# A gated attention and convolution block on one core: raw results of the first three projection pairs, their 1/rms applied in the output projections, and new due stages for the operands of the second half

## The chip, the core and the metric

The kernel runs on one core of one Trainium2 chip. The metric is the device time of one execution in microseconds (us); lower is better. The core's engines are named as in the profile: PE is TensorE (matmuls; PEld its weight loads), DVE is VectorE, ACT is ScalarE, POOL is GpSimd, SP is SyncE, which only issues DMAs. Each engine works through its own queue in order. ACT issues some DMAs too.

## The reference

`x` has 2048 tokens of 1024 features. All is float32. Cut to what matters:

```python
def rmsnorm(x, g):
    r = lax.rsqrt(jnp.mean(x * x, axis=-1, keepdims=True) + EPS)
    return (x * r) * g

h = rmsnorm(x, norm_g)
proj = h @ w_in            # 1024 x 6144
q, k, v, z_att, gb, gc, u, z_conv, g_att, g_conv = split(proj)
att = chunked_rel_attention(q, k, v, rel_bias)   # 64-token chunks, 8 chunks back, 8 heads
y_att = (att * silu(z_att)) @ w_att_out
vconv = causal_depthwise_conv(gc * u, conv_w, conv_b)
y_conv = (gb * vconv * silu(z_conv)) @ w_conv_out
m = sigmoid(g_att) * y_att + sigmoid(g_conv) * y_conv
x = x + m @ w_out
out = rmsnorm(x, final_norm_g)
```

The 6144 columns of `w_in` are 512 each for q to z_conv, and 1024 each for the two gates. Since 1/rms is one factor for each token, it can be applied to `x` before the projection or to the projection's result after it.

## The kernel before, in words

**Number format.** Each float32 operand is split into a high and a low part (`split_into`, `split_pair`): ACT casts the high part (L127, L133), DVE subtracts it from the source to get the low part (L128, L134). A product of two operands takes three matmul passes (`passes`, L140 to L142): high by high, high by low, low by high.

**The projection.** The tokens are worked in two halves of 1024, each in two chunks `c` of 512 columns. The weight columns are worked in 24 pairs `p` of two 128-column tiles `n`. A pair of tiles by two chunks of tokens is a 2x2 block product, done in Strassen's form with Winograd's additions: seven products instead of eight, in the order `ORDER = (1, 2, 6, 7, 4, 5, 3)`. Each product is a "stage": 12 matmuls (four tiles of 128 rows by three passes) into one bank of PSUM. Its operands are combinations of the token blocks, t1 to t7 (tiles t10h, t10l to t73l; built by `operand_steps`, one product's operands for each step), and combinations of the weights (`operand`: tiles `wc`, out of raw weights `wraw`, loaded in pairs). The weight combinations of half 0 are stored in DRAM (the `wc` stores) and loaded again for half 1 (L383), except those of the first three pairs in the order.

**The plain pairs.** Half 0 begins before 1/rms is known. Its first three pairs (`PLAIN = 3`, gate columns d = 0 to 2 of g_att and g_conv, tiles `n` = 0 and 1) are computed without Strassen on tokens that are multiplied by the norm's gain only (`raw_split`): 12 products `q`, each of 24 matmuls, into banks `ps_p`. Meanwhile the sums of squares and 1/rms are made (`rb`, one tile for each chunk), and DVE normalizes the tokens (`normalize`, `third`). The results of the first four plain products are copied by ACT; those of the others stay in their bank. Each is then multiplied by 1/rms on DVE (`scaled`, L654), after which `ev_gate` does a tanh on ACT (L416) and stores the gate through ACT's own DMA queue (L417). In between, operand steps of half 0 (t1, t2, t6, t7, t4) and the first weight combinations are built. All this is under a schedule written by hand for PE, DVE and ACT, so the order of the code is the order on the engines.

**The change of halves.** The last pair of half 0 (z columns) and the pair before it are interleaved, then the first two pairs of half 1 (`ending`, `beginning`). In these, the operands t1 to t7 are rebuilt from the tokens of half 1, into slots that half 0's operands leave. `turned = operand_steps(1)` is advanced one step each time a stage `s` reaches the first entry of the list `due`. Before, each of the last pair's seven stages adds an entry two stages later. With S the stage of the first product of the last pair, the steps come at S + 3, 4, 5, 7, 9, 11 and 13. The last z results (`sz`, L468, on DVE) are stored by SP (L474), in the same queue as the loads of `wc` (L383) and of raw weights (L375).

**Attention** runs among the projection stages of half 1: scores (`ps_s`), softmax (`nmax`, `rs`, `pr`), transposes, `pt` split into parts on ACT and DVE (L219, L220), and the product with `vv` (L229). At the end of half 1's projections the attention and convolution results of half 0 (`mid`) are loaded by SP into operand slots that come free.

**The output projections** (`half_c`, one for each half of the tokens) go through 16 items (i, d) in the order of `ITEMS_C`: i = 1 is the convolution branch, i = 0 attention, d a 128-column tile. For each item, weights `wy` are split, two gate tiles `gl` are loaded by SP from `gate_d` (L558, a pool of five buffers), and one product of 12 matmuls runs for each chunk. DVE then forms (gate + 1) x product (L960, L963) and adds the two branches (L964). Jobs for the next part, W_out's product in `half_d`, are worked off between: splits of W_out's tiles (`wor`, L903 and L904) and of m (`mix`, L926, L927). PSUM holds three banks for these products.

## Time and profile before

| | |
|---|---|
| time, three runs | 1504.21 us median (1502.57 to 1506.2) |
| the profiled execution's own time | 1508.27 us |
| its span in the trace | 1506.5 us |
| mean granted clock of PE | 0.995 |
| PE busy | 1475.3 us, 98% |
| DVE busy | 1090.5 us, 72% |
| ACT busy | 740.1 us, 49% |
| DMA | 408.28 MB, mean 271 GB/s |

How to read it: times in the trace are us from the span's start. A row of a timeline has the start, the duration, the engine, the line of the kernel, the operation, out<-in with the buffer numbers left out, and the shapes; in square brackets stand the engine's idle time before it and what ended it. "x2" at the end means that two such instructions follow each other without a gap. A row of the waits has the waiting engine and line, the engine and tile that ended the wait, then the us in total, how many times, and the longest. A row of the windows has the stretch, its length, the busy time of each engine asked for with the number of instructions, the granted clock of PE as a share of full speed, the mean share of the DMA engines' time, and GB/s. "DMA to landing" is the time from the issue of a DMA to its landing.

### The profile page before, as it was taken

How to read it: one execution, taken by the hardware profiler on the slowest of the kernel's cores; microseconds unless marked ns; L12 is line 12 of the kernel's file. 1: busy time of each engine (PE TensorE's matmuls, PEld its weight loads, DVE VectorE, ACT ScalarE, POOL GpSimd, SP SyncE). 2: the span in 40 equal slices, each digit the busy share in tenths (PEclk: the TensorE clock that was granted, in tenths of full speed). 3: DMA queues.
4: the chain of work that ended last, by engine and by line, in shares of the span. 5: the costliest groups of instructions: out<-in, count | busy, mean ns of one | idle time of the engine just before them, and what ended most of it. 6: DMA issues, size and time to landing. Idle time of an engine off the chain costs nothing. (4 is left out here: it accounts for less than half of the span.)

```text
span 1506.5 us, 21077 instructions
## 1 busy us (share of the span) xinstructions
PE 1475.3 (98%) x6976; PEld 1226.2 (81%) x6976; DVE 1090.5 (72%) x2121; ACT 740.1 (49%) x1399; POOL 163.8 (11%) x310
## 2 busy tenths in 40 slices
PE   8899999999999999999999999999999999999997
PEld 6778888888877788887888888888888888888886
DVE  7977588596557784676677777787765577767687
ACT  7363453444345333565566666666666223423153
POOL 0000000000000002232222323322220000010000
PEclk9999999999999999999999999999999999999999
DMA  5279899989988895999898887878989845877443
GB/s 214 73 273 352 308 361 351 348 295 328 345 304 287 314 341 173 339 341 337 288 295 286 259 260 249 265 256 264 310 282 314 307 129 168 294 262 240 153 162 112
DMA packets 168748, 408.28 MB, mean 271 GB/s; under 512 B 21056, under 2 KB 41536, under 8 KB 168640
## 3 DMA queue, kind: packets, MB, share of 16 engines
q1 hardware_dynamic: 137008, 316.48, 60.7%
q0 software_dynamic: 22272, 73.42, 15.4%
q10 hardware_dynamic: 9360, 17.04, 3.1%
q8 instruction: 55, 0.90, 0.2%
q14 instruction: 53, 0.43, 0.1%
HBM read 251.67 MB, written 155.19 MB: 270 GB/s over the span
## 5 line engine op out<-in xcount | busy, mean ns | idle before, releaser
L162 POOL DMA_DIRECT2D q<-q x128 | 66.8, 527 | 675.5 <-DVE wc L128 585.0
L204 ACT ACTIVATE pr<-ps_s,nmax 128x640 f32<-128x640 f32 (+4 forms) x128 | 93.5, 730 | 93.0 <-DVE nmax L200 92.3
L206 ACT ACTIVATE pr<-pr,rs 128x640 f32<-128x640 f32 (+4 forms) x128 | 97.9, 765 | 35.3 <-DVE rs L205 34.9
L200 DVE CUSTOM_DVE_ANT_0 ps_s<-ps_s,bs 128x640 f32<-128x640 f32 (+4 forms) x128 | 95.3, 744 | 23.7 <-PE ps_s L194 22.4
L140 PE MATMUL ps_d<-mid,wy 128*128 128x512 f32 x256 | 99.7, 389 | 0.8 <-ACT wy L127 0.8
L128 DVE TENSOR_TENSOR wc<-wraw,wc 128x512 fp32r<-128x512 f32 x120 | 82.3, 688 | 24.7 <-ACT wc L127 24.5
L141 PE MATMUL ps_d<-mid,wy 128*128 128x512 f32 x256 | 99.6, 389 | 0.0
L194 PE MATMUL ps_s<-kk,q 128*128 128x320 f32 (+1 forms) x448 | 98.5, 334 | 1.0 <-ACT pr L204 0.5
L142 PE MATMUL ps_d<-mid,wy 128*128 128x512 f32 x256 | 99.3, 389 | 0.0
L220 DVE TENSOR_TENSOR pt<-ps_t,pt 128x640 fp32r<-128x640 f32 (+4 forms) x128 | 94.1, 735 | 3.4 <-ACT pt L219 2.5
L127 ACT CAST wc<-wraw 128x512 fp32r<-128x512 f32 x120 | 74.1, 621 | 44.2 <-PE ps_c L142 23.0
L219 ACT CAST pt<-ps_t 128x640 fp32r<-128x640 f32 (+4 forms) x128 | 80.1, 626 | 21.9 <-PE ps_t L214 20.7
L214 PE MATMUL ps_t<-ident,pr 128*128 128x128 f32 x560 | 82.3, 273 | 0.2
L229 PE MATMUL po<-pt,vv 128*128 128x512 f32 x336 | 75.5, 356 | 4.1 <-DMA vv<-v 3.2
L229 PEld LDWEIGHTS po<-pt,vv 128*128 128x128 f32 x336 | 62.1, 188 | 19.1 <-issue 3.5
L214 PEld LDWEIGHTS ps_t<-ident,pr 128*128 128x128 f32 x560 | 65.7, 140 | 9.9 <-issue 1.5
L194 PEld LDWEIGHTS ps_s<-kk,q 128*128 128x128 f32 x448 | 67.6, 190 | 5.6 <-ACT pr L204 4.8
L997 PE MATMUL ps_w<-wo,lefth 128*128 128x512 f32 (+1 forms) x240 | 71.9, 382 | 0.0
L140 PEld LDWEIGHTS ps_d<-mid,wy 128*128 128x128 f32 x256 | 48.0, 188 | 11.1 <-ACT wy L127 1.2
L234 DVE TENSOR_TENSOR ot<-po,ot 64x256 f32<-64x256 f32 x64 | 26.6, 415 | 41.3 <-ACT ot L233 40.4
L141 PEld LDWEIGHTS ps_d<-mid,wy 128*128 128x128 f32 x256 | 48.0, 188 | 10.1
L142 PEld LDWEIGHTS ps_d<-mid,wy 128*128 128x128 f32 x256 | 48.1, 188 | 9.9
(535 smaller groups left out, 4110.4 us busy)
## 6 DMA issues: line engine op xcount, KB each, us to landing
wc<-wc SPq DMA_DIRECT2D x294, 512.0 KB, 5.3
wraw<-wp_in SPq DMA_DIRECT2D x54, 512.0 KB, 5.8
q<-q POOLq DMA_DIRECT2D x128, 128.0 KB, 5.0
gl<-gate SPq DMA_DIRECT2D x64, 256.0 KB, 2.8
mid<-mid SPq DMA_DIRECT2D x64, 256.0 KB, 5.3
wor<-wo SPq DMA_DIRECT2D x56, 256.0 KB, 5.2
bs<-bias POOLq DMA_DIRECT2D x32, 320.0 KB, 7.7
v<-vst SPq DMA_DIRECT2D x64, 128.0 KB, 4.6
```

The source lines that it names most:

```text
L128: nc.vector.tensor_sub(w[:, 1], src, w[:, 0].bitcast(F32))
L140: nc.tensor.matmul(ps, lhsT=w[:, 0, k, :], rhs=rh[:, cs], start=(first and not onto and k == 0), stop=False, skip_group_check=onto)
L141: nc.tensor.matmul(ps, lhsT=w[:, 0, k, :], rhs=rl[:, cs], start=False, stop=False, skip_group_check=onto)
L142: nc.tensor.matmul(ps, lhsT=w[:, 1, k, :], rhs=rh[:, cs], start=False, stop=(last and k == len(rhs) - 1), skip_group_check=onto)
L194: nc.tensor.matmul(ps[:, i, :m], lhsT=q[s][:, g * P:(g + 1) * P], rhs=kk[:, k1 - n + i * m:k1 - n + (i + 1) * m], start=(s == 0), stop=(s ...
L200: nc.vector.tensor_tensor_reduce(out=view, in0=view, in1=bv, scale=-0.125, scalar=3.0e38, op0=ALU.add, op1=ALU.min, accum_out=nmax)
L204: nc.scalar.activation(out, view, AF.Exp, bias=nmax, scale=-1.0, accum_out=rs)
L206: nc.scalar.activation(pr[:, :n], pr[:, :n], AF.Identity, scale=rs)
L214: nc.tensor.transpose(out=ps[:, j * P:(j + 1) * P], in_=pr[:, j * P:(j + 1) * P], identity=ident)
L219: nc.scalar.copy(hi[:, js, qs], src)
L220: nc.vector.tensor_sub(lo[:, js, qs], src, hi[:, js, qs].bitcast(F32))
L229: nc.tensor.matmul(ps[:, :, a * P:b * P], lhsT=vv[:, g0 + j, :], rhs=pt[:, j, :, a * P:b * P], start=(i == 0), stop=(i == len(js) - 1))
```

## The change

Three things.

1. The 12 plain results are no longer multiplied by 1/rms and no longer go through `ev_gate`. ACT copies each out of its bank, and SP stores it raw in `plain_d`. SP also stores the two tiles of 1/rms (`rb_d`).
2. In `half_c` of the first half, for items with d < 3, the loaded raw gate is multiplied by 1/rms on DVE and goes through the tanh on ACT, in place. The two 1/rms tiles (`rbs`) are loaded by SP into operand slots, ahead of the first `mid` loads. `ITEMS_C` and the order of `mix` are rearranged.
3. `due` is set once, from the list `TURN`. The seven steps in `ORDER`'s order come at S + 3, 4, 6, 9, 13, 16 and 18.

```diff
+TURN = (2, 3, 5, 8, 12, 15, 17)
...
+    plain_d = [dram.tile([P, CH], F32, name=f"plain{q}") for q in range(4 * PLAIN)]
+    rb_d = [dram.tile([P, CH], F32, name=f"rb{c}") for c in range(2)]
...
     def gate(i, d, c):
         g = gp.tile([P, CH], F32, tag="g", name="gl")
-        nc.sync.dma_start(g, gate_d[i][d][c])
+        nc.sync.dma_start(g, plain_d[plain.index((d, i, c))] if unscaled(d, c) else gate_d[i][d][c])
         return g
 
-    ITEMS_C = [(i, d) for dd in ((0, 4, 1, 5), (2, 6, 3, 7)) for i in (1, 0) for d in dd]
+    def unscaled(d, c):
+        return d < PLAIN and c < 2
+
+    ITEMS_C = [(i, d) for dd in ((3, 7, 0, 4), (1, 5, 2, 6)) for i in (1, 0) for d in dd]
...
-    def scaled(p, n, c, src):
-        t = src if src.space != PSUM else e("c")
-        nc.vector.tensor_mul(t, src, rb[c])
-        late.append(lambda: evs[p][n](c, c, t))
...
-        if q in (6, 7):
-            for n in range(2):
-                copied.pop(0)()
         if q > 5 and len(built) < 5:
             built.append(next(steps))
...
                 rb[0] = inverse(ry[0], e)
+                store(rb_d[0], rb[0])
...
                     rb[1] = inverse(ry[1], e)
+                    store(rb_d[1], rb[1])
                 passes(ps, wops0[p, n, k], [raw_ops[c, 4 * k + j] for j in range(4)], slice(0, CH), k == 0, k == 1)
-            if q < 4:
-                t = e("plain")
-                nc.scalar.copy(t, ps)
-                copied.append(lambda p=p, n=n, c=c, t=t: scaled(p, n, c, t))
-            else:
-                now, late = late, []
-                between(q)
-                if q > 4:
-                    scaled(*held0)
-                held0 = (p, n, c, ps)
-                for fn in now:
-                    fn()
+            t = e("plain")
+            nc.scalar.copy(t, ps)
+            store(plain_d[q], t)
+            between(q)
...
-        scaled(*held0)
-        for fn in late:
-            fn()
...
                 turned = operand_steps(1)
-            due.append(s + 2)
+                due = [s + d for d in TURN]
...
             made = make_c(0, ITEMS_C[0])
+            rbs = [fslot("rbs") for c in range(2)]
+            for c in range(2):
+                nc.sync.dma_start(rbs[c], rb_d[c])
             mids = {c: [load_mid(1, b, c) for b in range(4)] for c in (0, 1)}
...
             split_into(w, raw)
+            if d < PLAIN and not hf:
+                for c in cs:
+                    nc.vector.tensor_mul(gl[c], gl[c], rbs[c])
+                    nc.scalar.activation(gl[c], gl[c], AF.Tanh, scale=0.5)
...
             if n_ in (7, 10, 14, 15):
-                mix((7, 10, 14, 15).index(n_))
+                mix((3, 0, 1, 2)[(7, 10, 14, 15).index(n_)])
```

In the changed kernel the line numbers are three higher in the first part of the program, and from the plain stage on about ten to thirteen lower: L133 becomes L136, L468 becomes L471, and L798 becomes L785. TensorE runs the same matmuls in both.

The order of the instructions changes at these places, among others. On ACT in the plain stage, between the casts of t6 and t7 for half 0, this stands before (plain and c are results of plain products, "DMA gate" is a store that ACT issues):

```order
L133 CAST t63h<-xs 128x512
L416 ACTIVATE plain<-plain 128x512
L417 DMA gate_0_1_156<-plain 128x512
L416 ACTIVATE plain<-plain 128x512
L417 DMA gate_0_1_188<-plain 128x512
L416 ACTIVATE c<-c 128x512
L417 DMA gate_1_1_160<-c 128x512
L133 CAST t70h<-xs 128x512
L133 CAST t71h<-xs 128x512
L133 CAST t72h<-xs 128x512
L133 CAST t73h<-xs 128x512
```

And this in the changed kernel:

```order
L136 CAST t63h<-xs 128x512
L714 COPY plain<-ps_p 128x512
L136 CAST t70h<-xs 128x512
L136 CAST t71h<-xs 128x512
L136 CAST t72h<-xs 128x512
L136 CAST t73h<-xs 128x512
L714 COPY plain<-ps_p 128x512
L136 CAST t40h<-xs 128x512
```

The tanh and the stores have left the queue, and copies out of the banks ps_p stand there.

On DVE at the change of halves, near the end of half 0, this stands before (sz and v are z results of half 0; t4, t5 and the tiles t1 belong to the operands of half 1):

```order
L815 TENSOR_TENSOR v_4827<-v_4827,ps_c_4695 128x512
L134 TENSOR_TENSOR t43l_4808<-xs_1580,t43h_4807 128x512
L362 TENSOR_TENSOR t1_4851<-xs_1586,xs_1577 128x512
L468 SCALAR_TENSOR_TENSOR sz_4830<-sz_4830,v_4827 128x512
L468 SCALAR_TENSOR_TENSOR sz_4848<-sz_4848,ps_c_4433 128x512
L134 TENSOR_TENSOR t50l_4854<-t1_4851,t50h_4853 128x512
L362 TENSOR_TENSOR t1_4857<-xs_1586,xs_1577 128x512
L362 TENSOR_TENSOR t1_4863<-xs_1586,xs_1577 128x512
L362 TENSOR_TENSOR t1_4869<-xs_1586,xs_1577 128x512
L134 TENSOR_TENSOR t51l_4860<-t1_4857,t51h_4859 128x512
L468 SCALAR_TENSOR_TENSOR sz_4890<-sz_4890,ps_c_4546 128x512
```

And this in the changed kernel:

```order
L802 TENSOR_TENSOR v_4807<-v_4807,ps_c_4675 128x512
L137 TENSOR_TENSOR t73l_4788<-xs_1583,t73h_4787 128x512
L361 TENSOR_TENSOR xs_1580<-xs_1580,xs_1577 128x512
L471 SCALAR_TENSOR_TENSOR sz_4810<-sz_4810,v_4807 128x512
L471 SCALAR_TENSOR_TENSOR sz_4828<-sz_4828,ps_c_4433 128x512
L471 SCALAR_TENSOR_TENSOR sz_4846<-sz_4846,ps_c_4546 128x512
L137 TENSOR_TENSOR t40l_4873<-xs_1580,t40h_4872 128x512
```

The last three sz now stand ahead of t4, and t5 follows later in the queue.

On DVE near the end of half 1, among the softmax of attention, this stands before:

```order
L220 TENSOR_TENSOR pt_5674<-ps_t_11636,pt_5674 128x5x128
L205 RECIPROCAL rs_11652<-rs_11652 128x1
L200 ISA ps_s_11681,nmax_11686<-ps_s_11681,bs_11501 128x2x320
L200 ISA nmax_11686 128x1
L220 TENSOR_TENSOR pt_5674<-ps_t_11673,pt_5674 128x5x128
```

And this in the changed kernel, where gl is a raw gate and rbs the tile of 1/rms:

```order
L223 TENSOR_TENSOR pt_5674<-ps_t_11636,pt_5674 128x5x128
L208 RECIPROCAL rs_11652<-rs_11652 128x1
L938 TENSOR_TENSOR gl_11992<-gl_11992,rbs_11881 128x512
L203 ISA ps_s_11681,nmax_11686<-ps_s_11681,bs_11501 128x2x320
L203 ISA nmax_11686 128x1
L223 TENSOR_TENSOR pt_5674<-ps_t_11673,pt_5674 128x5x128
```

The first of the twelve new multiplications stands there. The others are in the output projections of the first half.

On SP in the plain stage, the store of each plain result stands in its own turn: those of the fifth to the eighth result and of the second tile of 1/rms are ahead of the two raw weight loads of the fifth pair, or between them.

More of the change, by code (lines that the diff above doesn't have):

```diff
@@ L642, in block_kernel @@
     plain = [(p, n, c) for p in range(PLAIN) for c in range(2) for n in range(2)]
-    copied = []
-    late = []
     nw = 0
```

## Prediction

> **What bounds the kernel now.** I read the page's first part, then TensorE's waits, then every gap of TensorE on its timeline, then windows of 4 us around the gaps.
>
> ```profile
> span 1506.5 us, 21077 instructions
> PE 1475.3 (98%) x6976; PEld 1226.2 (81%) x6976; DVE 1090.5 (72%) x2121; ACT 740.1 (49%) x1399; POOL 163.8 (11%) x310
> ```
>
> TensorE (PE) works for 1475.3 of 1506.5 us, so the span is its work plus 31.2 us of gaps. The change leaves all matmuls, so it can only win or lose gaps, and time in which the clock is low. The waits say who ends the gaps (us in total, times, longest):
>
> ```profile
> PE ps_p L140 <- DVE c L654: 4.7, 2, 2.9
> PE ps_c L140 <- ACT wc L127: 4.4, 2, 3.2
> ```
>
> The first row and the longest of the second lie in the plain stage, before 90 us. On PE's timeline these and the gaps at the change of halves are:
>
> ```profile
> 58.66 0.66 PE L140 MATMUL ps_p<-rawh,w 128*128 128x512 f32 x1 [1.86 <-DVE c L654]
> 74.27 0.50 PE L140 MATMUL ps_p<-rawh,w 128*128 128x512 f32 x1 [2.87 <-DVE c L654]
> 88.65 0.50 PE L140 MATMUL ps_c<-t10h,wc 128*128 128x512 f32 x1 [3.16 <-ACT wc L127]
> ...
> 493.61 0.50 PE L140 MATMUL ps_c<-t30h,wc 128*128 128x512 f32 x1 [0.54 <-ACT v L814]
> 503.26 0.50 PE L140 MATMUL ps_d<-t20h,wc 128*128 128x512 f32 x1 [0.90 <-DMA wc<-wc]
> 510.84 0.47 PE L140 MATMUL ps_d<-t20h,wc 128*128 128x512 f32 x1 [1.80 <-ACT t33h L133]
> ```
>
> So the change touches two places, with 1.86 + 2.87 + 3.16 = 7.89 us and 0.54 + 0.90 + 1.80 = 3.24 us of gaps. The granted clock (the column PEclk, third from the end) answers to some gaps:
>
> ```profile
> 56.00:60.00 4.00, 2.14 (x8) 0.85 0.30 113
> 60.00:64.00 4.00, 4.00 (x15) 0.73 0.64 197
> 72.00:76.00 4.00, 1.73 (x8) 1.00 0.35 130
> 88.00:92.00 4.00, 3.35 (x9) 0.69 0.90 208
> 92.00:96.00 4.00, 4.00 (x17) 0.89 0.99 385
> ```
>
> After the gap of 1.86 us, 4 x (0.15 + 0.27) = 1.68 us of clock are lost; after that of 3.16 us, 4 x (0.31 + 0.11) = 1.68 us; after that of 2.87 us none. The first loss is hidden, since PE then waits for VectorE anyway; the second is paid.
>
> **Part 1, the plain stage.** The question is when the first Strassen product (88.65 us) can start. It needs t1 to t4 and its weights, all out of one chain on VectorE (DVE) and ScalarE (ACT).
>
> ```profile
> 76.53 0.69 DVE L134 TENSOR_TENSOR t70l<-xs,t70h 128x512 fp32r<-128x512 f32 x1 [2.32 <-ACT t70h L133]
> ...
> 78.95 0.69 DVE L654 TENSOR_TENSOR c<-ps_p,rb 128x512 f32<-128x512 f32 x1
> 79.55 0.68 DVE L358 TENSOR_TENSOR xs<-xs 128x512 f32<-128x512 f32 x1
> ```
>
> ```profile
> 86.96 0.62 ACT L416 ACTIVATE c<-c 128x512 f32<-128x512 f32 x1
> ...
> 87.98 1.14 ACT L127 CAST wc<-wraw 128x512 fp32r<-128x512 f32 x2 [0.40 <-ACT c L416]
> ```
>
> By the order rows shown with the change, three tanh with their DMA issues have gone from ahead of t70h on ACT, for one copy. The terms:
> - Twelve multiplications L654 leave DVE, nine of them ahead of t43l; one row starts 0.60 us after the one before (78.95, 79.55). 9 x 0.60 = -5.4 us.
> - The wait of 2.32 us for t70h, which those three tanh made, goes: the copy in their place belongs to a product that has ended by then. -2.3 us.
> - A tanh and its issue stand ahead of the weight cast that PE waits for: 87.98 - 86.96 = -1.0 us.
> - The copy of the eighth product stands ahead of t20h and holds t2 back: +0.7 us, an estimate.
> - A new wait. The raw weights of the fifth pair are loaded when the last plain weights are split, before here:
>
> ```profile
> 59.75 5.74 SPq L375 DMA_DIRECT2D wraw<-wp_in  x2
> ```
>
> The second went out 0.3 us before the end of these 5.74 us, at 65.2; with seven of the multiplications gone ahead of it and the 0.7 us it is 65.2 - 4.2 + 0.7 = 61.7 now. SyncE's queue (SP) is in order, and four plain stores (plain4 to plain7) and a store of 1/rms are queued ahead of those two loads. I cost them at nothing: the last needs the copy of the eighth product, which ends at 58.66 - 1.86 = 56.8, plus 0.6 for the copy. Loads of wraw take this long here, between 50 and 80 us and between 40 and 130 us:
>
> ```profile
> DMA to landing us min/median/max: 3.6/3.7/3.7
> ...
> DMA to landing us min/median/max: 3.6/6.2/7.3
> ```
>
> With 3.7 us the pair lands at 65.4; DVE, counted on at 0.60 us a row, comes to it (L392) at 64.6, and t6 and t4 are queued behind it. I take +0.9 us (0 to 4.4, with 7.3).
>
> Sum: -5.4 - 2.3 - 1.0 + 0.7 + 0.9 = -7.1 us; the product of 88.65 us starts at 81.5. PE itself would now be there earlier: without waits at 58.66 and 74.27, since ACT empties the banks by then, the last four plain products run on from 56.8, 24 matmuls or 5.44 us each (twice the product measured in part 3), to 78.6. A gap of some 2.9 us stays. If the clock drops after it, the 1.68 us are paid as before, and the gain is 7.1; if not, it is 8.8. Gaps of 1.86 and 3.16 us had a drop, the one of 2.87 none: I take the drop, as the gap is nearest in its place and releaser to the one of 3.16.
>
> The Trainium skill (TensorE: Matmul & The Clock Gate, Part 1) has the clock halved after an idle window of about 3.4 us, windows running freely. Half rate for 3.4 us is the measured 1.7 us. But it also says that idle gaps only matter above 3.4 us, and the gaps of 1.86 and 3.16 us here speak against that; by its rule the sum of this part would be 8.8, which is a rival below.
>
> **Part 2, the change of halves.** The operand steps of half 1 were due two stages after each product of the last pair, now at fixed stages with the later ones (t4, t5, t3) further out.
>
> ```profile
> 505.00:510.00 5.00, 5.00 (x10) 1.00 0.93 334
> ```
>
> ```profile
> 502.68 0.32 SPq L474 DMA_DIRECT2D z<-sz  x1
> ...
> 504.06 0.38 SPq L383 DMA_DIRECT2D wc<-wc  x1
> ```
>
> ```profile
> 506.16 0.69 DVE L468 SCALAR_TENSOR_TENSOR sz<-sz,ps_c 128x512 f32<-128x512 f32 x1
> ```
>
> DVE (second number) never rests there. The z results wait in its queue behind operands, SP's z stores wait for them, and weight loads stand behind those stores. The gap at 510.84 is named after t33h, which that product doesn't read; its weights were issued at 504.06. By DVE's order rows at the change of halves, the last sz moves up past t5, t4 and the tiles t1: counted in the whole order by eleven rows (11 x 0.60 = 6.6 us), the third last by six (3.6 us). With the store of that one the load of 504.06 moves to about 500.5. Its weights then land 3.6 us earlier, more than the 1.80 us that PE waited. Since PE arrives earlier too, I leave 1.0 of the 3.24 us standing: -2.2 us (-3.2 to -0.5). What is deferred is needed late: half 1's first pair runs two products for each of t1, t2, t6, t7 and t4 before it reads t5 and t3.
>
> **Part 3, what is added later.** Two loads of 1/rms stand on SP ahead of the loads of the attention results, and wait for the first operand slots to come free:
>
> ```profile
> 1143.47 1.37 SPq L553 DMA_DIRECT2D mid<-mid  x3
> ```
>
> ```profile
> 1146.88 0.83 DVE L200 CUSTOM_DVE_ANT_0 ps_s<-ps_s,bs 128x640 f32<-128x640 f32 x1 [1.46 <-PE ps_s L194]
> ...
> 1147.63 0.82 DVE L220 TENSOR_TENSOR pt<-ps_t,pt 128x640 fp32r<-128x640 f32 x1
> ```
>
> ```profile
> 1149.43 1.30 PE L229 MATMUL po<-pt,vv 128*128 128x512 f32 x6
> ```
>
> The loads of mid, in 1140 to 1165 us:
>
> ```profile
> DMA to landing us min/median/max: 4.0/5.5/8.5
> ```
>
> ```profile
> 1156.00:1162.00 6.00, 5.18 (x26) 4.09 (x26) 3.02 (x7) 2.78 (x5) 0.00 (x0) 1.00 1.03 390
> ```
>
> The first new multiplication needs rbs, issued at 1143.47: it lands at 1143.47 + 5.5 = 1149.0, and, as DVE's order rows show, the row's max (L203) and pt (L223), which the matmuls of 1149.43 read, are queued behind it. By the two DVE rows pt starts 0.75 us after the max and takes 0.82: it ends at 1149.0 + 0.6 + 0.75 + 0.82 = 1151.2, and PE waits 1.8 us (0.3 with 4.0, 4.8 with 8.5). As the first of these loads may be near the fastest, I take +1.4. The 0.5 MB more, where the DMA engines are full (1.03, 390 GB/s), take 1.3 us of them; most of it runs beside that wait: +0.2. Together +1.6 us (0 to 4.8).
>
> In half 0's output projections DVE gets 12 multiplications (7.2 us) and ACT 12 tanh, beside a full PE:
>
> ```profile
> 1196.85 0.69 DVE L963 SCALAR_TENSOR_TENSOR gl<-gl,ps_d 128x512 f32<-128x512 f32 x1 [1.47 <-PE ps_d L142]
> ...
> 1207.59 0.68 DVE L963 SCALAR_TENSOR_TENSOR gl<-gl,ps_d 128x512 f32<-128x512 f32 x1
> ```
>
> ```profile
> 1195.21 0.86 SPq L896 DMA_DIRECT2D wor<-wo  x2
> ```
>
> The loads of wor, in 1190 to 1200 us:
>
> ```profile
> DMA to landing us min/median/max: 2.8/4.7/5.1
> ```
>
> ```profile
> 519.12 0.39 PE L140 MATMUL ps_d<-t70h,wc 128*128 128x512 f32 x1
> ...
> 521.84 0.39 PE L140 MATMUL ps_d<-t70h,wc 128*128 128x512 f32 x1
> ```
>
> A product of 12 matmuls takes 521.84 - 519.12 = 2.72 us, and three banks let DVE lag by two products, 5.44 us. Before, the fourth of these rows came at 1207.59, 2.6 us after its product (1196.85 + 3 x 2.72 = 1205.0); with its 0.69 us, 2.1 us of slack are left. Now a split of W_out's tiles (wor) has moved to right behind the first row and waits for its load (1195.21 + 4.7, then a cast), until about 1201 us; two multiplications come before the fourth row too. Counted on at 0.60 us a row, I get it done 0.9 us before PE needs the bank. So nothing if all is in time, and 2.1 us if the loads are slow: +0.4.
>
> **The sum.** -7.1 - 2.2 + 1.6 + 0.4 = -7.3 us. The profiled execution took 1508.27 us (span 1506.5 and 1.77 around it), so it would be 1501.0; that run is 4.06 above the median of the runs shown (1504.21), and against the median it is 1496.9. I call over 0.2% of it (3.0 us) a difference, about what a measurement of this kernel can tell.
>
> **Rivals.**
> - *No drop of the clock after the new gap.* For it: 2.87 us passed without one. Against: 1.86 and 3.16 did not. 1496.9 - 1.7 = 1495.2. The rule of the Trainium skill's page on the clock gate gives this time too.
> - *The raw pair lands late.* If plain stores and wide loads share the DMA engines and it takes 7.3 us, DVE waits 3.6 us more ahead of t6: 1500.5. Against: 3.7 was the longest in this stretch.
> - *Given back at the end of half 1 and after.* With 4.8 and 2.1 us: -7.1 - 2.2 + 6.9 = -2.4, 1501.8, no difference. For it: full DMA engines.
> - *Slower: DVE's queue stands still in half 0's output projections.* Each multiplication waits for its own gate load:
>
> ```profile
> gl<-gate SPq DMA_DIRECT2D x64, 256.0 KB, 2.8
> ```
>
> If the four between 1196 and 1216 us each cost a whole load and themselves, with 3 us for wor, that is 4 x (2.8 + 0.6) + 3.0 - 2.1 of slack = 14.5 us on PE; -7.7 + 14.5 = +6.8, 1511.0. It decides once DVE stands for more than 2.1 us there, and makes the kernel slower past 2.1 + 7.7 + 3.0 = 12.8. Against: five buffers let SP issue a load two products ahead.
>
> **How the numbers follow.** Forecast 0.46, the clock 0.27, the late pair 0.11, given back 0.10, slower 0.06. The two first and the late pair are faster by over 3.0 us, with a little less than that for misses at the edges: faster 0.84, same 0.10, slower 0.06. The low end is -8.8 - 3.2 with nothing given back, 1492.2; the high end is the case given back with the smallest gain at the change of halves (-7.1 - 0.5 + 6.9 = -0.7, 1503.5) less 1.0, as all at once is unlikely: 1502.5. What lies above is the slower case and half of its neighbour.
>
> **What would show it.** Right: no gap behind L140 ps_p after 50 us; the first ps_c near 81.5 with a gap of 2 to 3.5 us; DVE without a wait of 2.32 us at t7; gaps at the change of halves near 1 us; one new gap near 1143 us behind pt. Wrong: a DVE wait for wraw of several us near 65; gaps between 1197 and 1225; t5 or t3 as a releaser after the change of halves.

## The result, and the profile after

| | before | changed |
|---|---|---|
| time, six runs each, median | 1504.72 us (1502.57 to 1506.2) | 1498.75 us (1497.69 to 1501.38) |
| the profiled execution's own time | 1508.27 us | 1499.37 us |
| its span | 1506.5 us | 1497.6 us |
| mean granted clock | 0.995 | 0.997 |

Ratio 0.9964, interval 0.9951 to 0.9977: faster, by 5.4 us (3.5 to 7.4). Forecast were 7.3 us and 1496.9; the measured median lies 1.9 us above that, 0.5 of it because the median of before over six runs is 1504.72 and not 1504.21.

The head of the page after, the same rows as were shown of before:

```profile
span 1497.6 us, 21082 instructions
PE 1475.1 (99%) x6976; PEld 1224.8 (82%) x6976; DVE 1091.9 (73%) x2121; ACT 745.2 (50%) x1407; POOL 163.9 (11%) x310
```

PE's busy time is the same to 0.2 us (1475.3 before); only its gaps have shrunk, from 31.2 to 22.5 us. Its longest waits now (us in total, times, longest):

```profile
PE ps_c L143 <- ACT wc L130: 4.0, 2, 2.8
PE ps_d L143 <- DMA wc<-wc: 2.2, 1, 2.2
```

The waits for ps_p that DVE's multiplications ended (4.7 us) are gone. The places on PE's timeline:

```profile
81.06 0.50 PE L143 MATMUL ps_c<-t10h,wc 128*128 128x512 f32 x1 [2.76 <-ACT wc L130]
...
501.51 0.64 PE L143 MATMUL ps_d<-t20h,wc 128*128 128x512 f32 x1 [2.16 <-DMA wc<-wc]
...
1139.90 1.44 PE L232 MATMUL po<-pt,vv 128*128 128x512 f32 x6 [0.70 <-DVE pt L223]
```

In the plain stage one gap is left where there were three (1.86, 2.87, 3.16). At the change of halves one is left too, but it is longer than any of the three there before (0.54, 0.90, 1.80). One new gap stands at the attention row behind the added loads, as forecast, of 0.70 us.

Where the time went can be read by cutting both executions at the starts of the same PE instructions and subtracting. All numbers are us.

| stretch | its end (a start on PE), before and changed | length before | changed | difference |
|---|---|---|---|---|
| to the first plain product | 8.27, 8.00 | 8.27 | 8.00 | -0.27 |
| to the first Strassen product | 88.65, 81.06 | 80.38 | 73.06 | -7.32 |
| most of half 0 | 468.23, 460.62 | 379.58 | 379.56 | -0.02 |
| to t2 after the change of halves | 510.84, 501.51 | 42.61 | 40.89 | -1.72 |
| right behind that | 547.68, 539.91 | 36.84 | 38.41 | +1.57 |
| attention | 966.64, 956.18 | 418.96 | 416.27 | -2.69 |
| end of half 1 | 1172.01, 1162.09 | 205.37 | 205.91 | +0.54 |
| half 0's output projections | 1238.58, 1229.99 | 66.57 | 67.90 | +1.33 |
| the rest | | 267.88 | 267.61 | -0.27 |

The -2.69 of the attention stretch is not the change's. In this execution of before, PE waited there once for `vv` and lost clock after it:

```profile
720.03 0.59 PE L229 MATMUL po<-pt,vv 128*128 128x512 f32 x2 [1.84 <-DMA vv<-v]
```

```profile
720.00:724.00 4.00, 3.97 (x15) 0.62 1.05 352
```

Over the twelve profiles of this study the same stretch took 413.9 to 419.0 us, whatever the edit. Without it the sum is -8.86 + 2.69 = -6.2 us, which is close to the timed difference of the medians (-6.0).

### The profile page after: what moved, and what is told of

It is laid out like the page before. It is cut to its first block, busy times and chain, and to the rows that moved or that the text cites. A ratio compares the mean times of both kernels' runs of the same rounds, so it can differ in the third digit from the quotient of the medians.

```text
span 1497.6 us, 21082 instructions
## 1 busy us (share of the span) xinstructions
PE 1475.1 (99%) x6976; PEld 1224.8 (82%) x6976; DVE 1091.9 (73%) x2121; ACT 745.2 (50%) x1407; POOL 163.9 (11%) x310
## 5 line engine op out<-in xcount | busy, mean ns | idle before, releaser
L217 PEld LDWEIGHTS ps_t<-ident,pr 128*128 128x128 f32 x560 | 65.6, 140 | 10.2 <-issue 1.4
L893 ACT ACTIVATE wo<-wor 128x512 fp32r<-128x512 f32 x56 | 34.3, 629 | 52.6 <-DMA wor<-wo 41.7
L143 PEld LDWEIGHTS ps_d<-mid,wy 128*128 128x128 f32 x256 | 48.0, 188 | 12.8 <-ACT wy L130 1.2
L130 ACT CAST wc<-s 128x512 fp32r<-128x512 f32 x48 | 29.8, 621 | 53.5 <-PE ps_d L145 40.0
L145 PEld LDWEIGHTS ps_d<-mid,wy 128*128 128x128 f32 x256 | 48.1, 188 | 10.1
```

The source lines that it names most:

```text
L130: nc.scalar.copy(w[:, 0], src)
L143: nc.tensor.matmul(ps, lhsT=w[:, 0, k, :], rhs=rh[:, cs], start=(first and not onto and k == 0), stop=False, skip_group_check=onto)
L145: nc.tensor.matmul(ps, lhsT=w[:, 1, k, :], rhs=rh[:, cs], start=False, stop=(last and k == len(rhs) - 1), skip_group_check=onto)
L217: nc.tensor.transpose(out=ps[:, j * P:(j + 1) * P], in_=pr[:, j * P:(j + 1) * P], identity=ident)
```

## The experiments

Each kernel was timed beside the kernel before on one chip; the ratio is against those runs of before, whose median was 1506.0 to 1506.5 us. Diffs are against the changed kernel unless said.

### The two parts apart

**e1, the plain stage's part alone.** The due stages are the old ones.

```diff
-                due = [s + d for d in TURN]
+            due.append(s + 2)
```

> The changed kernel with the old due stages: only the plain results' part of the change. Theory (all of the gain comes from the plain stage, the new due stages gave nothing, since the weights at 501.5 us landed late in full DMA engines): the first Strassen product starts at 81.1 us as in the changed kernel, the gaps at the change of halves are those of before (0.5, 0.9 and 1.8 us), and the time is within 1 us of the changed kernel's 1498.75. Rival (the forecast's, the new due stages are worth 2.2 us): 2.2 us more than the changed kernel, 1501.

Measured: 1498.56 us, ratio 0.9957 (0.9942 to 0.9973). The gap ahead of the first Strassen product, and the clock after it (third number from the end):

```profile
81.17 0.50 PE L143 MATMUL ps_c<-t10h,wc 128*128 128x512 f32 x1 [2.67 <-ACT wc L130]
```

```profile
80.00:84.00 4.00, 2.83 (x12) 1.00 0.37 101
```

The changed kernel's windows at the same place:

```profile
80.00:84.00 4.00, 2.94 (x8) 0.72 0.41 118
84.00:88.00 4.00, 4.00 (x16) 0.85 1.02 390
```

The same gap, to 0.1 us, once without and once with a drop of the clock; the last section shows what decides it. The drop costs 4 x (0.28 + 0.15) = 1.7 us there. So the first rival (no drop) and the forecast are not two theories of the kernel: an execution falls to one or the other.

The gaps at the change of halves in e1:

```profile
484.52 0.50 PE L143 MATMUL ps_c<-t30h,wc 128*128 128x512 f32 x1 [0.53 <-ACT v L801]
...
493.89 0.50 PE L143 MATMUL ps_d<-t20h,wc 128*128 128x512 f32 x1 [0.62 <-DMA wc<-wc]
...
501.59 0.47 PE L143 MATMUL ps_d<-t20h,wc 128*128 128x512 f32 x1 [1.96 <-DMA wc<-wc]
```

They are those of before, to 0.3 us. The plain part alone gives as much time, within the intervals, as the whole change.

**e2, the change of halves' part alone.** Against the kernel before:

```diff
-            due.append(s + 2)
+                due = [s + d for d in (2, 3, 5, 8, 12, 15, 17)]
```

> The kernel before with the new due stages alone. Theory: of the gaps at the change of halves the first two (0.5 and 0.9 us) go, one of about 2 us stays at the second product of t2, named after a load of wc; the time is within 1 us of before. Rival (the forecast's): 2.2 us faster than before.

Measured: 1503.79 us, ratio 0.9994 (0.998 to 1.0007): no difference that the runs can tell. The profile does show one: the gaps of 0.54 and 0.90 us are gone, the stretch to t2 takes 40.52 instead of 42.61 us, and this gap stays:

```profile
507.02 0.47 PE L140 MATMUL ps_d<-t20h,wc 128*128 128x512 f32 x1 [1.79 <-DMA wc<-wc]
```

So the part does what it says to the operands (counted from the last pair's first product itself, their steps now come 2, 3, 5, 8, 12, 15 and 17 stages later, the entries of `TURN`; the S of the text ahead of the prediction is one stage before that product), and what stays is a wait for weights. The 2.1 us of the profile are within the interval of the ratio (-3.0 to +1.1 us), so the times neither show nor exclude them.

### The plain stage: what the 7.3 us are made of

**e6, no multiplication and nothing else.** Against the kernel before. The tanh reads the bank, and the gates d < 3 of half 0 stay without 1/rms.

```diff
-        t = src if src.space != PSUM else e("c")
-        nc.vector.tensor_mul(t, src, rb[c])
-        late.append(lambda: evs[p][n](c, c, t))
+        late.append(lambda: evs[p][n](c, c, src))
```

> The kernel before without the 12 multiplications by 1/rms: the first three pairs' gates of the first half go through the tanh unscaled. Theory: the first Strassen product starts at 88.65 - 5.4 = 83.3 us (up to 0.9 more for the raw weights), about 5 us faster than before. Rival (with the multiplications gone ACT's tanh become the bound, so that the two only gain together): it starts at 86 us or later.

Measured: 1507.60 us, ratio 1.0012 (1.0 to 1.0023). Not one of the 5.4 us that the nine multiplications were costed at came out. PE's timeline:

```profile
70.94 0.80 PE L140 MATMUL ps_p<-rawh,w 128*128 128x512 f32 x1 [9.05 <-ACT c L416]
```

And ACT's:

```profile
67.71 0.62 ACT L133 CAST t63h<-xs 128x512 fp32r<-128x512 f32 x1 [1.91 <-DVE xs L356]
...
70.29 0.60 ACT L416 ACTIVATE c<-ps_p 128x512 f32<-128x512 f32 x1 [0.40 <-ACT plain L416]
```

The bank is now freed by the tanh, which stands in ACT's queue behind t6's casts, and these wait for DVE. PE waits 9.05 us for a bank; the first Strassen product starts at 90.95, later than before (88.65). The theory of "DVE's multiplications alone" (83.3) fell, and the rival, that ACT becomes the bound, held: the multiplications also freed the banks early.

**e5, the tanh moved and the multiplications kept.** The multiplications stay where they were in before, from the banks for q > 3; the tanh is in the output projections, and there is no `rbs`.

```diff
+    def scaled(q, c, src):
+        t = src if src.space != PSUM else e("c")
+        nc.vector.tensor_mul(t, src, rb[c])
+        store(plain_d[q], t)
...
-            t = e("plain")
-            nc.scalar.copy(t, ps)
-            store(plain_d[q], t)
-            between(q)
+            if q < 4:
+                t = e("plain")
+                nc.scalar.copy(t, ps)
+                copied.append(lambda q=q, c=c, t=t: scaled(q, c, t))
+            else:
+                between(q)
+                if q > 4:
+                    scaled(*held0)
+                held0 = (q, c, ps)
...
-                    nc.vector.tensor_mul(gl[c], gl[c], rbs[c])
```

> The changed kernel, but the plain results are still multiplied by 1/rms on DVE in the plain stage (as before) and then stored by SP; only the tanh and ACT's DMA issues have moved to the output projections. It tells the terms of the plain stage apart. Theory (DVE's multiplications are worth 5.4 us, ACT's tanh and issues 3.3 us, as the forecast's sum has them): the first Strassen product starts at 88.65 - 3.3 = 85.3 us, and the time is about 3.5 us above the changed kernel's. Rival (the multiplications alone held the chain, the tanh ran beside it): it starts at 88 us, no gain over before.

Measured: 1504.69 us, ratio 0.9997 (0.9986 to 1.0008). ACT's chain came earlier by 87.98 - 84.43 = 3.55 us:

```profile
84.43 1.14 ACT L130 CAST wc<-wraw 128x512 fp32r<-128x512 f32 x2
...
1054.67 0.63 ACT L948 ACTIVATE gl<-gl 128x512 f32<-128x512 f32 x1 [3.54 <-DMA gl<-plain]
```

But PE was not there to use all of it. It had stood here, waiting for a bank that DVE empties:

```profile
74.16 0.50 PE L143 MATMUL ps_p<-rawh,w 128*128 128x512 f32 x1 [4.35 <-DVE c L659]
```

The first Strassen product started at 86.82, between the theory's 85.3 and the rival's 88, with no gap ahead of it: PE's own plain products, which DVE's multiplications still held up, were the bound. The time of the whole says nothing on this, since the version loses elsewhere: the tanh that now waits 3.54 us for its gate at 1054 holds the softmax behind it in ACT's queue (PE gaps of 1.30 us at 1056.13 and 0.68 us at 1060.40).

**e10, the banks freed by ACT, the multiplications kept.** As e5, but ACT copies all twelve results, and DVE multiplies the copies in place.

```diff
+    def scaled(q, c, t):
+        nc.vector.tensor_mul(t, t, rb[c])
+        store(plain_d[q], t)
...
             nc.scalar.copy(t, ps)
-            store(plain_d[q], t)
-            between(q)
+            if q < 4:
+                copied.append(lambda q=q, c=c, t=t: scaled(q, c, t))
+            else:
+                between(q)
+                if q > 4:
+                    scaled(*held0)
+                held0 = (q, c, t)
...
-                    nc.vector.tensor_mul(gl[c], gl[c], rbs[c])
```

> The changed kernel with the 12 multiplications by 1/rms back on DVE in the plain stage, at their old places in its queue, but on the copies that ACT made, so that the banks are free at once. Theory (the nine multiplications ahead of t4 delay the operand chain by 9 x 0.60 = 5.4 us less about 1 us of waits for the raw weights that they fill; the banks had been a second bound of the plain products): the last plain product ends at 78.3 us as in the changed kernel, and the first Strassen product starts at 85.4 to 86.5 us. Rival (the multiplications only mattered by holding the banks): it starts at 81.1 to 82 us.

Measured: 1506.58 us, ratio 1.0002 (0.9988 to 1.0017), with a loss later, as in e5 (a tanh waits 4.52 us for its gate at 1055.25, and PE stands 2.24 us and loses clock). The plain stage can be read:

```profile
85.06 0.61 PE L143 MATMUL ps_c<-t10h,wc 128*128 128x512 f32 x1 [4.23 <-ACT wc L130]
```

PE waits for the chain again, not for a bank, and the theory's 85.4 is met to 0.4 us. With the multiplications kept, freeing the banks by ACT is worth 86.82 - 85.06 = 1.8 us (e5 against e10). Against before and the changed kernel, e10 splits the gain: 88.65 - 85.06 = 3.6 us for what left ACT, and 85.06 - 81.06 = 4.0 us for the multiplications off DVE, with the new waits paid.

**e4, the last gap filled.** 11 matmuls whose result nobody reads run after the last plain product.

```diff
+        fill = bank("fill")
+        t10 = ops[0, 1, 0][0]
+        for _ in range(11):
+            nc.tensor.matmul(fill, lhsT=t10[:, :P], rhs=t10, start=True, stop=True)
```

> The changed kernel with 11 matmuls of 128x512 on t1's first tile, whose result nobody reads, between the last plain product and the first Strassen product (2.5 us of work in a gap of 2.76 us). Theory (the gap makes the clock drop, and the drop costs 1.7 us): the granted clock stays at 1.00 from 80 to 88 us and the time falls by 1.7 us, to 1497.0. Rival (a gap under 3.4 us does no harm and the drop has another cause): the clock drops as before (0.72 and 0.85), no change of time.

Measured: 1497.49 us, ratio 0.9948 (0.9932 to 0.9963). The clock stays whole:

```profile
80.00:84.00 4.00, 3.93 (x17) 1.00 0.32 99
84.00:88.00 4.00, 4.00 (x19) 1.00 1.01 384
```

From the first Strassen product to the same point of half 0 it took 346.35 us, as in e1 (346.06), against 347.66 in the changed kernel's profile and 347.67 in before's, which both lost clock there. This drop is worth 1.3 to 1.6 us in these profiles; the times of e4 and of the changed kernel overlap and don't tell. That before paid it too is why half 0 shows no difference between the two traces.

### The change of halves: why the gap of 2.16 us stays

**e3, the raw weights loaded later.** SyncE's queue has two loads of 512 KB (raw weights) right ahead of the weights that PE waits for. They are put behind the later loads of `wc` here.

```diff
-        if i == 1 and n in (NPAIR, *range(NPAIR + 2, NPAIR + 1 + PLAIN)):
+        if (n, i) == (NPAIR, 7) or i == 1 and n in range(NPAIR + 2, NPAIR + 1 + PLAIN):
```

> The changed kernel, but the first two raw weight loads of the second half (1 MB) are issued some stages later, behind the loads of wc that the first products wait for. Theory (bytes ahead in the DMA queue hold the weights back): the weights awaited at 501.5 us land about 2.6 us earlier (1 MB at 400 GB/s), the gap of 2.2 us goes and with it the low clock of 0.66 behind it (1.4 us): 3.6 us less than the changed kernel, 1495.2. Rival (the loads are held by SP's queue or by a slot, not by bytes): the gap stays and the time is that of the changed kernel.

Measured: 1495.85 us, ratio 0.9939 (0.9921 to 0.9957). SyncE's queue in the changed kernel:

```profile
491.96 1.37 SPq L378 DMA_DIRECT2D wraw<-wp_in  x2
493.43 0.39 SPq L386 DMA_DIRECT2D wc<-wc  x1
```

And in e3:

```profile
491.85 0.84 SPq L386 DMA_DIRECT2D wc<-wc  x1
...
502.32 1.72 SPq L378 DMA_DIRECT2D wraw<-wp_in  x2
```

The raw loads go out 10.4 us later, and the awaited load, the fourth of L386 in the program's order in both, goes out 1.6 us earlier (491.85 and 493.43). In the changed kernel it lands after

```profile
DMA to landing us min/median/max: 7.9/7.9/7.9
```

and in e3 after

```profile
DMA to landing us min/median/max: 5.6/5.6/5.6
```

So it lands at 497.43 instead of 501.37, 3.9 us earlier, where the theory had 2.6. PE has no gap at the change of halves any more, and no drop behind it. The changed kernel's windows, and then e3's:

```profile
500.00:505.00 5.00, 3.49 (x9) 0.66 1.04 416
```

```profile
500.00:505.00 5.00, 5.00 (x24) 1.00 1.01 397
```

The stretch to t2 takes 38.54 us (40.89 in the changed kernel, 42.61 before), the next one 36.72 (38.41, 36.84). Nothing but the place of these two loads was changed: without the raw loads ahead of that load of `wc` there is no wait. The intervals of the times of e3 and of the changed kernel (0.9951 to 0.9977) just overlap; the profile decides.

**e9, the raw weights later, with the old due stages.** e3's edit, and e1's.

> The changed kernel with the later raw loads and the old due stages. It asks what the new due stages are worth when no raw loads stand in front of the awaited weights. Theory (they do what the forecast said, and the raw loads hid it): against the kernel with later raw loads and new due stages, the gaps of 0.5, 0.6 and up to 2 us at the change of halves come back, 2 us slower in sum, 1498. Rival (the raw loads were all; the new due stages are worth nothing): no gaps, 1495.9.

Measured: 1499.27 us, ratio 0.9949 (0.9929 to 0.997). Only one gap is left there:

```profile
486.34 0.50 PE L143 MATMUL ps_c<-t30h,wc 128*128 128x512 f32 x1 [0.52 <-ACT v L801]
```

The stretch takes 39.41 us, against 38.54 in e3 and 38.81 in e8 (below). So once the weights come in time, the new due stages take 0.6 to 0.9 us off this stretch, not the 1.6 to 2.1 us that they take off without that (e1 to the changed kernel, before to e2); the theory of 2 us fell. The intervals of the times overlap and decide nothing here.

With e9 there are profiles for all four cases. The awaited load, the same one in all twelve, took from issue to landing (us):

| | old due stages | new due stages |
|---|---|---|
| raw loads ahead of it | 6.6, 6.5, 6.0 (before, e1, e6) | 7.9, 7.7, 8.8, 7.7, 7.4, 7.8 (changed, e2, e4, e5, e7, e10) |
| raw loads behind it | 3.9 (e9) | 5.6, 5.6 (e3, e8) |

Both move it: the two raw loads ahead add 2.3 to 2.5 us in the mean, and the new due stages, by which it goes out some 3 us earlier, 1.5 to 1.7 us.

### The late part

**e7, without the loads of 1/rms, and the multiplications and tanh in the output projections.** The gates of d < 3 in half 0 are then left raw.

```diff
-            rbs = [fslot("rbs") for c in range(2)]
-            for c in range(2):
-                nc.sync.dma_start(rbs[c], rb_d[c])
...
-            if d < PLAIN and not hf:
-                for c in cs:
-                    nc.vector.tensor_mul(gl[c], gl[c], rbs[c])
-                    nc.scalar.activation(gl[c], gl[c], AF.Tanh, scale=0.5)
```

> The changed kernel without the loads of 1/rms, the 12 multiplications and the 12 tanh in the first half's output projections: the raw gates go in as they are. Theory (what was added late costs 0.5 us at 1140 to 1162 us and 1.3 us at 1186 to 1225): 1.8 us less than the changed kernel, the wait for pt at 1139.9 and the shifts from 1187 us on gone. Rival (they are hidden, and these shifts come from the new order of the items): no more than 0.3 us less, the shifts stay.

Measured: 1499.59 us, ratio 0.9953 (0.9935 to 0.9971): not faster than the changed kernel (0.9964). The times don't settle it: the clock was low for 10.2 us of e7's profile between the first and the last 15 us, for 6.8 us of the changed kernel's, which is worth 1.7 us. Half 0's output projections took 66.59 us, 1.3 less than in the changed kernel's profile, as expected; but e1, e3, e4 and e9, which have the same multiplications and loads, took 66.55 to 66.56. So the 1.33 us are not a standing cost of the added work. In the changed kernel's profile loads came late to DVE:

```profile
1190.92 0.69 DVE L894 SCALAR_TENSOR_TENSOR wo<-wor,wo 128x512 fp32r<-128x512 f32 x1 [2.81 <-ACT wo L893]
1193.67 0.69 DVE L938 TENSOR_TENSOR gl<-gl,rbs 128x512 f32<-128x512 f32 x1 [1.46 <-DMA gl<-plain]
```

The same two waits in e1:

```profile
1189.70 0.69 DVE L894 SCALAR_TENSOR_TENSOR wo<-wor,wo 128x512 fp32r<-128x512 f32 x1 [1.98 <-ACT wo L893]
1191.40 0.69 DVE L938 TENSOR_TENSOR gl<-gl,rbs 128x512 f32<-128x512 f32 x1 [0.40 <-DMA gl<-plain]
```

The two waits are 0.83 + 1.06 = 1.9 us longer together in the changed kernel's profile, more than the 0.9 us of slack that the forecast counted for DVE there. PE did wait for DVE, which e1's PE did not:

```profile
1195.71 0.47 PE L143 MATMUL ps_d<-mid,wy 128*128 128x512 f32 x1 [0.30 <-DVE gl L957]
```

Only 0.30 us of the 1.33 are named as a wait. Set beside e1's one by one, PE's starts fall back in three places: by about 0.4 us at 1186.3 to 1187.3, by 0.5 us with this gap, and by 0.3 us at 1201.5. The first lies ahead of DVE's two waits: there the weights `wy` came late (ACT stood 9.69 us for their load, 8.71 in e1, and DVE got to them at 1185.62, 1184.46 in e1). So late loads fit all of it, the added gate loads at most some 0.8 us of it; that is argued from the rows, no run changed these loads alone. The standing cost of the late part is then the wait for pt near 1140 us (0.70 us in the changed kernel, 0.49 in e1, 0.29 in e9, none in e3 and e4) and little more.

### Put together

**e8.** The raw weights later (e3), the fill (e4), and the two loads of 1/rms behind the first 16 loads of `mid` instead of ahead of them.

```diff
-            rbs = [fslot("rbs") for c in range(2)]
-            for c in range(2):
-                nc.sync.dma_start(rbs[c], rb_d[c])
             mids = {c: [load_mid(1, b, c) for b in range(4)] for c in (0, 1)}
+            rbs = [fslot("rbs") for c in range(2)]
+            for c in range(2):
+                nc.sync.dma_start(rbs[c], rb_d[c])
```

> The changed kernel with the later raw loads at the change of halves, the 11 matmuls in the gap, and the loads of 1/rms behind the first 16 loads of attention and convolution results. Theory: the gains add up, 2.9 + 1.3 + 0.5 us less than the changed kernel: 1494.0, about 0.8% below before. Rival (waits for vv and for the output projections' loads take back what is won): 1496 or more.

Measured: 1494.22 us (1493.99 to 1496.72), ratio 0.993 (0.9916 to 0.9943), faster than both kernels.

```profile
span 1492.2 us, 21102 instructions
PE 1473.2 (99%) x6987; PEld 1224.7 (82%) x6987; DVE 1091.2 (73%) x2121; ACT 745.3 (50%) x1407; POOL 164.3 (11%) x310
```

PE works 1.9 us less than in the changed kernel, with 11 matmuls more: a higher clock (0.999) makes the same matmuls shorter. A gap of 0.69 us behind pt is there in this profile too, now at 1153.07. The end of half 1 took 205.48 us, and 205.38 to 205.91 in the changed kernel, e1, e3 and e4, so what the third edit adds can't be told from the spread.

## Why the prediction was right, and where it was off

**The plain stage: right in the sum and in the parts.** Forecast -7.1 us and a first Strassen product at 81.5; it came at 81.06 (81.17 in e1). The ACT part was put at 2.3 + 1.0 = 3.3 us, e10 has 3.6; the DVE part with its new waits at 5.4 - 0.7 - 0.9 = 3.8 us, e10 has 4.0. Beyond waits that before has as well, DVE's waits in the changed kernel are those forecast, and one that was not:

```profile
57.69 0.69 DVE L137 TENSOR_TENSOR t20l<-xs,t20h 128x512 fp32r<-128x512 f32 x1 [0.54 <-ACT t20h L136]
63.16 0.69 DVE L137 TENSOR_TENSOR t60l<-xs,t60h 128x512 fp32r<-128x512 f32 x1 [1.16 <-ACT t60h L136]
65.24 0.69 DVE L395 TENSOR_TENSOR s<-wraw 128x512 f32<-128x512 f32 x1 [0.78 <-DMA wraw<-wp_in]
...
70.81 0.69 DVE L137 TENSOR_TENSOR t70l<-xs,t70h 128x512 fp32r<-128x512 f32 x1 [0.31 <-ACT t70h L136]
```

The copy ahead of t20h costs 0.54 us (forecast 0.7), the raw pair 0.78 (0.9), and the wait of 2.32 us for t70h has become 0.31; the 1.16 us for t60h (0.69 in before) were not forecast. DVE waited 0.69 us for t61h in before and does not now, so the raw pair cost 0.1 us net where 0.9 were taken, and t60h 0.5: two misses that partly cancel in the sum. The rival "the raw pair lands late" (3.6 us more) did not come. What the account had as free, and e6 and e5 show was not, is PE's banks: it took ACT's copies of all twelve results for the rest to count. The prediction said so in half a sentence ("since ACT empties the banks by then"); it was a condition of the whole term.

**The clock after the gap: right for the profiled run, by chance.** The drop was forecast because the gap looked like the one before it. e1's gap of 2.67 us, at the same place and behind the same releaser, had none. Neither the forecast's reason nor the rival's decides it: what counts is how a gap lies against a beat of 3.41 us that differs from one execution to the next (last section). The Trainium skill (TensorE: Matmul & The Clock Gate, Part 1) gives the rule "no PE-idle gaps >~3.4µs"; the drops after gaps of 2.76 and 2.16 us here show that shorter gaps cost clock too.

**The change of halves: the step that failed.** The term was -2.2 us; the stretch gave -1.72, and +1.57, the drop of the clock, came right behind it. The failed step is "its weights then land 3.6 us earlier, more than the 1.80 us that PE waited". The issue did move, nearly as counted: from 504.06 to 493.43, of which 7.59 us come from everything ahead being earlier, so 3.0 us. But the landing is not a fixed time after the issue. Before, the load landed after

```profile
DMA to landing us min/median/max: 6.6/6.6/6.6
```

and now after 7.9 us, so it lands only 1.7 us earlier against the work around it. The two raw loads moved up with it and stayed right ahead of it, and the DMA engines were full (last number but one, 1.03; 0.93 behind its issue in before, at 505 to 510 us):

```profile
490.00:495.00 5.00, 5.00 (x24) 1.00 1.03 348
```

PE arrived 2.1 us earlier (at 501.51 - 2.16 us, 38.7 into this stretch, against 40.8 before: the gaps of 0.54 and 0.90 us are gone, and with them some slower starts behind them), so its wait grew: 1.80 - 1.7 + 2.1 = 2.2 us. e3 takes the two loads away from that place and the gap goes. That the load takes longer when it goes out earlier stands in the table of e9, with and without the raw loads ahead; why it does is open, and no run changed only what else was under way then. The price of a clock drop after this gap (the window of 0.66 above) was in no term. It is not certain either: the gaps of 1.96, 2.10 and 2.16 us here (e1, e4, changed) had a drop behind them, those of 2.06, 2.15 and 2.40 (e6, e5, e10) had none, and those of 1.79 and 1.80 (e2, before) had none. By growing the gap past these last, the change made a drop possible here.

**The late part: less than forecast.** Forecast +2.0 us. The load of `rbs` took 4.5 us (5.5 was the median used, 4.0 the fastest), and DVE stood for it:

```profile
1137.68 0.69 DVE L938 TENSOR_TENSOR gl<-gl,rbs 128x512 f32<-128x512 f32 x1 [2.65 <-DMA rbs<-rb]
```

PE then waited 0.70 us where 1.4 were taken; the stretch lost 0.54 (forecast 1.6). Over the profiles in which the clock stays whole there, it took 204.84 to 205.37 us without the added loads (before, e2, e6) and 205.38 to 205.91 with them (changed, e1, e3, e4), so a loss of about 0.5 us is likely, in ranges that touch. Half 0's output projections lost 1.33 us in this profile (forecast 0.4, up to 2.1) and nothing in four others: the mechanism of slack used up by late loads was the forecast's, and it is an accident of a run rather than a cost. The slower rival, DVE standing for a load at each multiplication, did not show: three of the twelve multiplications waited for their gate in the changed kernel's profile, 1.46 us at the longest.

**The sum.** -7.32 - 1.72 + 1.57 + 0.54 + 1.33 - 0.56 (half 0 and the ends) = -6.16 us in the profile without the attention stretch, against -7.3 forecast. The difference is at the change of halves: the clock drop, and 0.5 us less in the stretch itself; the late part gave back a little less in sum.

## What to carry over

Before costing operations that leave a busy engine, ask what else they do: here the multiplications also emptied PE's banks, and taking them away alone (e6) gained nothing, while once a cheap copy on another engine empties the banks, taking them away gains 4.0 us. A load that is issued earlier does not land earlier by as much when larger loads move up ahead of it in the queue; look at what stands right ahead, and move that away (putting two loads 10 us later took 2.4 us out of this stretch, the new due stages 1.7). Of a gap near 2 us on PE, count the clock as well as the gap: by the estimate below, about half of 1.7 us.

## What the runs showed of the hardware

**The clock drops on a beat of 3.41 us, after a beat in which PE was idle for more than half of it.** Leaving out the first and the last 15 us, the twelve profiles have 17 drops, all to 0.50, of 3.41 us or two or three times that (6.83 us in e7, 10.24 in e6). The drops of one execution begin a whole number of 3.41 us apart: in before at 58.78, 89.50 and 720.97 us, 9 and 185 of them, in the changed kernel at 81.80 and 501.64, 123 of them. So each execution can be cut into beats, stretches of 3.41 us at whose ends alone a drop begins, and the idle time in a beat tells whether one does. The changed kernel's gap of 2.76 us falls almost whole into one:

```profile
78.39:81.80 3.41, 0.73 (x3) 1.00 0.10 41
81.80:85.21 3.41, 3.41 (x9) 0.50 0.85 264
```

In e1 a beat ends at 79.51 us (its own drop, at 502.76, begins 124 beats later) and cuts the gap of 2.67 us in two:

```profile
76.10:79.51 3.41, 2.40 (x11) 1.00 0.82 311
79.51:82.92 3.41, 1.75 (x7) 1.00 0.14 29
82.92:86.33 3.41, 3.41 (x16) 1.00 1.00 350
```

Sixteen of the 17 drops follow a beat with 1.84 us or more of idle time on PE, and no such beat was followed by the whole clock; the most idle beat without a drop has 1.83 us (before, where the gap of 2.87 us is cut into 1.04 and 1.83). The one exception is e7's drop at 957.70, behind 1.59 us. Gaps that are neighbours add up: in e9, one of 1.54 us and most of one of 0.95 us share a beat, and a drop follows at 955.00. Where the beat lies against the program differs from one execution to the next. If any place is equally likely, a gap of g us, from 1.84 to 3.4, escapes with a chance of (3.68 - g) / 3.41: an estimate of 0.27 for 2.76 us and 0.45 for 2.16. In the profiles, the gaps of 2.55 to 2.76 us ahead of the first Strassen product had a drop in four of five, those of 1.96 to 2.40 us at the change of halves in three of six. A drop of one beat costs 0.5 x 3.41 = 1.7 us of PE's work.

**A load's time grows with what is queued ahead.** The same load of `wc` (512 KB) at the change of halves took 3.9 to 5.6 us without two loads of 512 KB right ahead of it, and 6.0 to 8.8 us with them.

**A queue that waits for a load holds all behind it.** In e5 and e10 a tanh of 0.63 us that waited 3.54 and 4.52 us for its gate held ACT's softmax; in e10 that made this gap on PE:

```profile
1056.70 0.85 PE L197 MATMUL ps_s<-kk,q 128*128 128x320 f32 x4 [2.24 <-ACT pr L207]
```

In the changed kernel PE has no gap of this kind at the same point of the program.
